# Block products of an FFN on unscaled activations, summed in PSUM, and one more group of them

## The chip, the cores and the metric

The kernel runs on one core of one Trainium2 chip. The metric is device time in microseconds. Three runs of the kernel before gave 1812.3, 1813.72 and 1814.33 us; the median, 1813.72 us, is the time to compare with. The engines are called PE (TensorE: matmuls), DVE (VectorE), ACT (ScalarE), POOL (GpSimd) and SP (SyncE, which here only issues DMAs).

## The reference, cut to what matters

A sequence of 512 rows of 1024 fp32 numbers passes through two layers. Each layer is an FFN, a mixer and a second FFN; the mixers are not touched by the change except in the order of their instructions. An FFN (width 2816) is:

```python
def _rmsnorm(x, gain):
    y = x * lax.rsqrt(jnp.mean(x * x, axis=-1, keepdims=True) + EPS)
    return y * gain
def _swiglu(h, w_gate, w_up, w_down):
    return (jax.nn.silu(h @ w_gate) * (h @ w_up)) @ w_down
# per layer, twice:
h = _rmsnorm(x, ffn_norm[layer])
x = x + 0.5 * _swiglu(h, ffn_w_gate[layer], ffn_w_up[layer], ffn_w_down[layer])
```

The factor rsqrt(...) is one number per row of x. It can be taken out of `h @ w`, and put on the product.

## The kernel before, in words

**Layout and precision.** x lies transposed in SBUF: eight tiles of 128 features x 512 rows. An fp32 product is made of three matmuls: each operand is split into a high part, rounded to the type fp32r by a cast on ACT, and a low part, the difference, by a subtraction on DVE; the products high x high, high x low and low x high are summed in PSUM. A weight tile is loaded (`raw`, 128x1024), split into a tile `whl`, and used from there. The activations of a stage are `hg` tiles, the split of x times gain, without the row factor; the factor, broadcast to 128 partitions, is the tile `rsB`, and is put on a product as it leaves PSUM.

**An FFN.** Its 22 blocks of 128 hidden columns are worked as 11 pairs (called groups here, q = 0 to 10). A plain group is four units (gate and up of two blocks), each of 8 k-tiles x 3 matmuls of 512 columns (`proj_tile`), emptied by a DVE multiplication with `rsB` (`evac`). From q = `CLASSIC` on, a group is worked as two units of block products (`pair`, one for gate and one for up). A unit takes the two 128-column blocks, both halves of the features and both halves of the rows as a 2x2 block product, and makes it from 7 products in the place of 8. For that it needs sums and differences of weight blocks (made by DVE in `feed`, then split: W1, W3, W4 and W2) and of activations (`TA`, `TB`, made in `blocks`). Each of the 7 products is 4 x 3 matmuls of 256 columns. Before the change `blocks` works on normalized activations: it makes them with `rsB`, makes TA and TB from them, and later makes them again, splits them, and overwrites the activation tiles h (called N) with them, so that all 7 products have the row factor inside. The 7 products are added up by DVE from PSUM with the help tiles p1, u2, u3. `CLASSIC = (3, 9)`: the first FFN (f0) uses block products for q = 9 and 10, the three others for q = 3 to 10.

Then silu and product (`gate`), a split, and the down projection in units of 24 matmuls of 512 columns, in batches of three groups (`GROUPS`), which stand between the units of the following groups. `LEAD = (3, 4)` puts three (f0: four) such down units ahead of the first block product. In `ffn_items` this order is written down.

**The order of the work.** All instructions are put in order when the program is built, by a planner (`Clock`, `cost`) that keeps a time for every engine from fixed costs. The main path emits matmuls; after every few of them, `tick` lets other threads put in work: first the feeder (weight loads and splits), then the threads by `PRIO`. A thread that needs an engine asks `on`: for PE it goes on when its inputs have been ready for `SLACK` (1.5 us in f0) by the planner's clock; for DVE when DVE is at most `BACKLOG` ahead. `side` says whether a PSUM bank can be had for such a thread, by the planner's time at which the bank was last read. On the chip each engine runs its instructions strictly in this order and waits on semaphores.

**S5 tables.** During f0 the thread `prep` makes tables for the first mixer (`s5_prepare`): eight steps `gains_of_inputs` and eight `gains_of_outputs`, each with DVE products, four small matmuls or transposes into a side bank (lines 1177 and 1213), an ACT copy and DMAs through SP's queue. The extra SBUF for block products, and the thread `blocks`, start when `prep` has ended (`extra` in `ffn`).

The profile gives line 205 for every operation (a helper issues them all), so groups are told apart by tiles: `ps` PSUM, `whl` and `wh` split weights, `gs` and `us` gate and up results, `p`, `u` the help tiles, `g`, `bt`, `kt` tiles of the tables.

Of the kernel before, what the change touches and what calls it, by code (L numbers as in the profile page):

```python
# [17 lines left out]
P = 128  # L18
S = 512
# [22 lines left out]
CLASSIC = (3, 9)  # L42
LEAD = (3, 4)
HOLD = (1, 0)
# [11 lines left out]
PRIO = {"evac": 0, "gate": 0, "small": 5, "prep": 6, "blocks": 6, "s5_bounce": 1, "s5_quarter": 0, "s5_gate": 0, "s5_eighth": 1,  # L56
# [52 lines left out]
class Clock:  # L109
# [140 lines left out]
class Builder:  # L250
    def __init__(self, ctx, tc, A, out, plan):
# [18 lines left out]
        self.f, self.rsB, self.h, self.ndone, self.reserve, self.then, self.final = None, None, None, 0, 0, None, False  # L270
        self.xhold, self.go = False, False
# [46 lines left out]
    def on(self, eng, *aps, ps=0):  # L318
        c = self.clk
        while True:  # L320
            r = c.ready(*aps)
            if eng == "PE":
                ok = r + SLACK[self.name] <= c.now
            elif eng == "DMA":
                ok = r <= c.now + 0.5
            else:
                ok = r <= c.now + 0.3 and c.t[eng] <= c.now + self.backlog
            if ok and (not ps or self.side(ps) is not None):
                return
            yield  # L330
# [414 lines left out]
    def ffn(self, f, gi, then, prepare=None):  # L745
# [4 lines left out]
        with ExitStack() as st:  # L750
# [7 lines left out]
            def extra():  # L758
# [4 lines left out]
                self.xhold, self.go = prep is None, False  # L763
# [3 lines left out]
            self.N, self.TA, self.TB, self.ndone = h, [], [], 0  # L767
            grown = False
            for key in ffn_items(f):
# [3 lines left out]
                if key[0] == "blocks":  # L773
# [4 lines left out]
                    self.go = True  # L778
# [20 lines left out]
                elif key[0] == "pair":  # L799
                    q, i = key[2:]  # L800
                    self.until(lambda: self.ndone == KD and len(self.TB) == 4)
                    if i == 0:
                        t = {"gs": self.pair(w, "gs")}
                        nc.scalar.activation(out=t["gs"], in_=t["gs"], func=AF.Silu)
                    else:
                        t["us"] = self.pair(w, "us")
                        self.add("gate", self.gate(t, g, q, [1] * 4, 1))
                        if q == NFF // 2 - 1:
                            self.give(*self.N, *self.TA, *self.TB)
                else:  # L810
# [27 lines left out]
    def evac(self, ps, t, tag, m, done):  # L838
        while not self.scaled():
            yield  # L840
        if t[tag] is None:
            yield from self.room(tag, 1)
            if t[tag] is None:
                t[tag] = self.ft.tile([P, 2, S], F32, tag=tag, name=self.n(tag), bufs=1)
            else:
                self.leave(tag)
# [22 lines left out]
    def blocks(self, h, gi, late):  # L869
# [5 lines left out]

        hold = HOLD[late]
        again, kept = range(max(0, 4 - hold)), {}

        def normalized(kk, tag):
            t = yield from self.grab(tag, F32)  # L880
            n = (t[:, 0], t[:, 1]) if tag == "hg" else (t[:, lo], t[:, hi])
            for i in range(2):
                yield from self.normed(n[i], 4 * i + kk, h, gi, late)
            return t, n

        for kk in range(4):
            tn, (n1, n2) = yield from normalized(kk, "raw" if kk in again else "hg")
# [7 lines left out]
            v.tensor_tensor(out=t4, in0=t2, in1=n2[:, a], op=ALU.subtract)  # L895
            if kk in again:
                self.give(tn)
            else:
                kept[kk] = tn, (n1, n2)
# [4 lines left out]
            self.give(rt)  # L904

        for kk in again[:2]:
            kept[kk] = yield from normalized(kk, "raw")
        self.xhold = self.xhold and len(kept) < 4
        for kk in (3, 2, 1, 0):
            while not self.go:  # L910
                yield
            if kk not in kept:
                kept[kk] = yield from normalized(kk, "raw")
                self.xhold = self.xhold and len(kept) < 4
            tn, n = kept[kk]
            for i in range(2):
                yield from self.split_steps(n[i], h[4 * i + kk])
                self.ndone += 1
            self.give(tn)
        self.reserve = 0  # L920

    def block(self, ps, t, at, rhs, c, prev=None):
        nc = self.nc
        for kk in range(4):
            w = slice(at + kk * P, at + kk * P + P)
            r = rhs[kk]
            a = nc.tensor.matmul(out=ps, lhsT=t[:, 0, w], rhs=r[:, 0, c], start=kk == 0, stop=False)
            if kk == 0:
                self.after(a, prev)
            nc.tensor.matmul(out=ps, lhsT=t[:, 0, w], rhs=r[:, 1, c], start=False, stop=False)  # L930
            a = nc.tensor.matmul(out=ps, lhsT=t[:, 1, w], rhs=r[:, 0, c], start=False, stop=kk == 3)
            self.tick()
        return a

    def pair(self, w, tag):
# [4 lines left out]
        add = lambda out, x, y, op=ALU.add: v.tensor_tensor(out=out, in0=x, in1=y, op=op)  # L940
        p1, u2, u3 = (self.ft.tile([P, 256], F32, tag=tag, name=self.n(tag), bufs=1) for tag in ("p1", "u2", "u3"))

        X = self.main_ps()
        a = self.block(X[:, lo], W1, 512, N[4:8], lo)
        self.block(X[:, hi], W1, 0, N[0:4], lo, a)
        self.give(W1)
        self.nc.scalar.copy(out=p1, in_=X[:, hi])
        dst = self.ftile(tag)
        add(dst[:, 0, lo], X[:, lo], p1)
        self.free(X)  # L950
        Y = self.main_ps()
        a = self.block(Y[:, lo], W3, 0, TA, lo)
        self.block(Y[:, hi], W3, 512, TA, hi, a)
        self.give(W3)
        add(u2, Y[:, hi], p1)
        add(dst[:, 0, hi], Y[:, lo], u2)
        Z = self.main_ps()
        a = self.block(Z[:, lo], W4, 512, N[4:8], hi)
        self.block(Z[:, hi], W4, 0, TB, lo, a)
        self.give(W4)  # L960
        add(u3, Z[:, hi], u2)
        add(dst[:, 1, hi], Y[:, lo], u3)
        self.free(Y)
        add(dst[:, 0, hi], Z[:, lo], dst[:, 0, hi])
        self.free(Z)
        V = self.main_ps()
        self.block(V[:, lo], W2, 0, TB, hi)
        self.give(W2)
        add(dst[:, 1, lo], u3, V[:, lo], ALU.subtract)
        self.free(V)  # L970
        return dst
# [73 lines left out]
    def s5_prepare(self, pool):  # L1045
# [115 lines left out]
        def gains_of_outputs(e):  # L1161
# [15 lines left out]
            yield from self.on("PE", g1, bmx, ps=1)  # L1177
# [23 lines left out]
        def gains_of_inputs(e):  # L1201
# [11 lines left out]
            yield from self.on("PE", bt, ps=1)  # L1213
# [877 lines left out]
```

## Time and profile before

| | |
|---|---|
| median of 3 runs | 1813.72 us |
| the profiled execution | 1810.71 us |
| its span, first to last instruction | 1808.7 us |
| busy: PE, DVE, ACT | 99%, 79%, 42% |
| mean granted clock of PE | 0.999 |
| matmuls | 10514 |
| block products: units, matmuls of 256 columns | 52, 4368 |
| HBM read, mean rate | 192.82 MB, 114 GB/s |

The profile is of one execution; its time of 1810.71 us is that of the whole execution, the span is what the profiler saw between the first and the last instruction. A busy PE is not PE at its peak: matmuls overlap, so their durations (392 ns for 512 columns) are longer than the time from one start to the next. A wait is named after the operation that released it.

### The profile page before, as it was taken

The numbers are of one execution on the slowest core, as the hardware profiler recorded it, in microseconds if no ns is written. First come the engines' busy times: TensorE is split into PE (matmuls) and PEld (weight loads), VectorE is DVE, ScalarE is ACT, GpSimd is POOL, SyncE is SP. The second block draws the span as 40 slices with busy tenths as digits, with TensorE's granted clock in tenths as the row PEclk, the third lists the DMA queues.
The fourth block names the chain that finished last, engine by engine and source line by source line (L and its number), as shares of the span: only waits on it lengthen the run. The fifth ranks groups of instructions, "written<-read, shape, count | busy, mean of one in ns | idle before, by whom it ended". The sixth has DMA issues, their size and how long they took to land.

```text
span 1808.7 us, 26795 instructions
## 1 busy us (share of the span) xinstructions
PE 1792.4 (99%) x10514; PEld 1564.3 (86%) x10514; DVE 1428.9 (79%) x2599; ACT 754.7 (42%) x1082; POOL 18.7 (1%) x35
## 2 busy tenths in 40 slices
PE   9999999999999999999999999999999999999999
PEld 7877888978878889999988999998888788999997
DVE  8989877878986878887777988775578678988864
ACT  4323423433574444343343444333466544434331
POOL 0000000000010000000000000000000000000000
PEclk9999999999999999999999999999999999999999
DMA  5247432337773223332422333332434422333331
GB/s 196 92 141 190 144 103 82 117 130 205 201 168 114 88 89 104 118 105 95 138 64 78 106 117 97 103 102 86 144 78 111 129 82 76 100 106 107 111 98 70
DMA packets 80749, 207.16 MB, mean 115 GB/s; under 512 B 18000, under 2 KB 30320, under 8 KB 79472
## 3 DMA queue, kind: packets, MB, share of 16 engines
q1 hardware_dynamic: 78032, 196.52, 34.6%
q0 software_dynamic: 2448, 8.91, 3.1%
q8 instruction: 83, 1.36, 0.3%
q14 instruction: 42, 0.34, 0.1%
q10 hardware_dynamic: 144, 0.02, 0.0%
HBM read 192.82 MB, written 12.60 MB: 114 GB/s over the span
## 4 chain that ended last, share of the span: by engine, by line
PE 88%; DVE 8%; DMA 2%; issue 1%; ACT 1%; SPq 0%; DVEq 0%; ACTq 0%
PE ps L205 88%; DVE whl L205 1%; DVE hg L205 1%; DVE us L205 1%; DVE ex L205 1%; DVE ssb L205 1%; DMA raw<-in_wglu_dram 0%; DMA prm<-prm 0%; DMA s5ys<-ys 0%; ACT whl L205 0%; DVE s5x L205 0%; DMA ssb<-acsd 0%; DVE sc L205 0%; ACT hg L205 0%; DMA raw<-in_wgu_dram 0%
## 5 line engine op out<-in xcount | busy, mean ns | idle before, releaser
L205 PE MATMUL ps<-hg,whl 128*128 128x512 f32 (+1 forms) x8688 | 1609.6, 345 | 5.5 <-DVE hg L205 2.5
L205 PEld LDWEIGHTS ps<-hg,whl 128*128 128x128 f32 x8688 | 1375.5, 190 | 203.8 <-issue 4.6
L205 ACT CAST whl<-raw 128x1024 fp32r<-128x1024 f32 x366 | 383.0, 1051 | 532.3 <-PE ps L205 323.4
L205 DVE TENSOR_TENSOR whl<-raw,whl 128x1024 fp32r<-128x1024 f32 x349 | 424.1, 1222 | 180.8 <-ACT whl L205 180.3
L205 DVE SCALAR_TENSOR_TENSOR x<-ps,x 128x512 f32<-128x512 f32 x128 | 87.1, 688 | 37.0 <-PE ps L205 35.4
L205 DVE TENSOR_TENSOR raw<-raw,raw 128x512 f32<-128x512 f32 (+1 forms) x182 | 111.3, 649 | 2.2
L205 ACT CAST hg<-us 128x512 fp32r<-128x512 f32 x88 | 52.1, 620 | 105.2 <-DVE us L205 104.9
L205 PE MATMUL ps<-hg,wh 128*128 128x256 f32 x624 | 83.4, 283 | 0.0
L205 ACT ACTIVATE gs<-gs 128x1024 f32<-128x1024 f32 x44 | 46.7, 1060 | 85.5 <-DVE gs L205 85.5
L205 PEld LDWEIGHTS ps<-hg,wh 128*128 128x128 f32 x624 | 78.6, 192 | 0.0
L205 DVE TENSOR_TENSOR raw<-raw 128x512 f32<-128x512 f32 (+1 forms) x78 | 46.6, 597 | 16.4 <-DMA raw<-in_wgu_dram 16.4
L205 ACT COPY p<-ps 128x256 f32<-128x256 f32 x52 | 19.3, 372 | 95.5 <-PE ps L205 86.1
L205 DVE TENSOR_TENSOR hg<-us,hg 128x512 fp32r<-128x512 f32 x88 | 57.9, 685 | 0.0
L205 DVE TENSOR_TENSOR us<-gs,us 128x1024 f32<-128x1024 f32 x44 | 53.6, 1219 | 0.4
L205 ACT ACTIVATE hg<-x,gains 128x512 fp32r<-128x512 f32 x48 | 33.6, 722 | 32.4 <-DVE x L205 30.0
L205 ACT CAST hg<-raw 128x512 fp32r<-128x512 f32 x58 | 34.4, 622 | 21.3 <-DVE raw L205 20.6
L205 DVE TENSOR_TENSOR hg<-raw,hg 128x512 fp32r<-128x512 f32 x58 | 38.1, 689 | 0.1
L205 DVE SCALAR_TENSOR_TENSOR hg<-x,gains,hg 128x512 fp32r<-128x512 f32 x48 | 34.9, 746 | 2.5 <-ACT hg L205 2.5
L205 DVE TENSOR_TENSOR wh<-raw,wh 128x512 fp32r<-128x512 f32 x52 | 35.7, 686 | 0.0
L205 DVE TENSOR_TENSOR us<-ps,rsB 128x512 f32<-128x512 f32 x40 | 28.9, 723 | 4.5 <-PE ps L205 4.4
L205 ACT CAST wh<-raw 128x512 fp32r<-128x512 f32 x52 | 32.0, 616 | 0.0
L205 DVE TENSOR_TENSOR acc<-acc,sq 128x512 f32<-128x512 f32 x42 | 29.0, 690 | 0.9
(264 smaller groups left out, 1100.0 us busy)
## 6 DMA issues: line engine op xcount, KB each, us to landing
raw<-in_wgu_dram SPq DMA_DIRECT2D x176, 512.0 KB, 3.6
raw<-in_wdn_dram SPq DMA_DIRECT2D x88, 512.0 KB, 3.6
raw<-in_wev_dram SPq DMA_DIRECT2D x16, 512.0 KB, 3.6
prm<-prm SPq DMA_DIRECT2D x8, 1024.0 KB, 6.9
raw<-in_wod_dram SPq DMA_DIRECT2D x12, 512.0 KB, 3.6
raw<-in_wevo_dram SPq DMA_DIRECT2D x8, 512.0 KB, 6.6
raw<-in_wodo_dram SPq DMA_DIRECT2D x8, 512.0 KB, 6.4
x<-in_xT_dram SPq DMA_DIRECT2D x8, 256.0 KB, 5.6
```

Source lines behind the costliest of these rows:

```text
L205: r = f(*args, **kw)
```

## The change

- `pair` reads the activation tiles as they are (gain, no row factor). The two products of `N` with W1 and the one with W4 are multiplied with `rsB` when DVE reads them from PSUM; TA and TB are still made from normalized activations, so the four other products need no factor. `blocks` no longer makes the normalized activations a second time and no longer writes them back to h.
- Results that are sums of products are accumulated in PSUM: the bank X first holds W1 N[0:4], is read (p1), and then has W1 N[4:8] added; the bank Y is read after each of three products that are added into it in turn. The sign of t4 is turned for this. The last product of a unit is emitted in the next unit, after two blocks of it, or after a down unit (`pending`).
- The first product of a unit no longer waits until all activations are made again; each product waits only until its own TA or TB is there. `blocks` gets priority 0 in the place of 6; a thread `evac` is put behind the others of its priority.
- `CLASSIC = (3, 8)`: f0 uses block products for q = 8 too. `LEAD = (0, 0)`.
- The PE steps of the tables wait for `PREP_SLACK` = 4.0 us in the place of 1.5, for their inputs and for the bank; `side` takes the slack into account for every thread.
- The planner's cost of an fp32r matmul is (n + 32) / 2400 us.
- `WIDE` is False for all FFNs: the wide form in `block` is not used.

```diff
-CLASSIC = (3, 9)
-LEAD = (3, 4)
-HOLD = (1, 0)
+CLASSIC = (3, 8)
+LEAD = (0, 0)
+
+WIDE = (False, False)
...
+PREP_SLACK = 4.0
-PRIO = {... "blocks": 6, ...
+PRIO = {... "blocks": 0, ...
...
             if kw["lhsT"].dtype == F32R:
-                return max(0.11, 0.0025 + n / 2400)
+                return (n + 32) / 2400
...
     def add(self, kind, gen):
-        i = next((i for i, (q, _) in enumerate(self.threads) if q >= p), len(self.threads))
+        i = next((i for i, (q, _) in enumerate(self.threads) if q > p or q == p and kind != "evac"), len(self.threads))
...
-    def on(self, eng, *aps, ps=0):
+    def on(self, eng, *aps, ps=0, slack=None):
+        slack = SLACK[self.name] if slack is None else slack
...
-                ok = r + SLACK[self.name] <= c.now
+                ok = r + slack <= c.now
...
-            if ok and (not ps or self.side(ps) is not None):
+            if ok and (not ps or self.side(ps, slack) is not None):
...
-    def side(self, n=1):
+    def side(self, n=1, slack=0.0):
-            ok = min(most - self.open[w], sum(t <= self.clk.now for t in self.freed[w]))
+            ok = min(most - self.open[w], sum(t + slack <= self.clk.now for t in self.freed[w]))
...
                 elif key[0] == "pair":
                     q, i = key[2:]
-                    self.until(lambda: self.ndone == KD and len(self.TB) == 4)
                     if i == 0:
-                        t = {"gs": self.pair(w, "gs")}
-                        nc.scalar.activation(out=t["gs"], in_=t["gs"], func=AF.Silu)
-                    else:
-                        t["us"] = self.pair(w, "us")
-                        self.add("gate", self.gate(t, g, q, [1] * 4, 1))
+                        t = {}
+                    last = self.pair(w, t, "us" if i else "gs", pending)
+
+                    def pending(last=last, t=t, q=q, i=i):
+                        last()
+                        if i == 0:
+                            nc.scalar.activation(out=t["gs"], in_=t["gs"], func=AF.Silu)
+                        else:
+                            self.add("gate", self.gate(t, g, q, [1] * 4, 1))
...
+                    if pending:
+                        pending()
+                        pending = None
...
     def blocks(self, h, gi, late):
-            tn, (n1, n2) = yield from normalized(kk, "raw" if kk in again else "hg")
+            tn = yield from self.grab("raw")
+            n1, n2 = tn[:, lo], tn[:, hi]
+            for i, n in enumerate((n1, n2)):
+                yield from self.normed(n, 4 * i + kk, h, gi, late)
...
-            v.tensor_tensor(out=t4, in0=t2, in1=n2[:, a], op=ALU.subtract)
+            v.tensor_tensor(out=t4, in0=n2[:, a], in1=t2, op=ALU.subtract)
...
-        for kk in again[:2]:
-            kept[kk] = yield from normalized(kk, "raw")
-        self.xhold = self.xhold and len(kept) < 4
-        for kk in (3, 2, 1, 0):
...
-            for i in range(2):
-                yield from self.split_steps(n[i], h[4 * i + kk])
-                self.ndone += 1
-        self.reserve = 0
+        self.xhold, self.reserve = False, 0

+    def block(self, ps, t, at, rhs, c, more=False, wide=False):
         for kk in range(4):
+            self.until(lambda: len(rhs) > kk)
...
+            first, last = kk == 0 and not more, kk == 3
...
+    def pair(self, w, t, tag, before):
...
         X = self.main_ps()
+        self.block(X, W1, 0, N[0:4], lo)
+        p1 = new("p1", 2)
+        times(p1, X[:, lo], lo)
+        Z = self.main_ps()
+        self.block(Z[:, hi], W4, 512, N[4:8], hi)
+        if before:
+            before()
+        t[tag] = dst = self.ftile(tag)
+        Y = self.main_ps()
+        self.block(Y, W3, 512, TA, hi, wide=wide)
+        plus(dst[:, 0, hi], Y, p1)
+        self.block(X, W1, 512, N[4:8], lo, more=True)
+        times(dst[:, 0, lo], X[:, lo], lo)
+        self.block(Z, W3, 0, TA, lo)
+        add(dst[:, 0, hi], Z[:, lo], dst[:, 0, hi])
+        p5 = new("p5", 1)
+        times(p5, Z[:, hi], hi)
+        add(dst[:, 0, hi], dst[:, 0, hi], p5)
+        self.block(Y, W4, 0, TB, lo, more=True, wide=wide)
+        plus(dst[:, 1, hi], Y, p1)
+        add(dst[:, 1, hi], Z[:, lo], dst[:, 1, hi])
+
+        def last():
+            self.block(Y, W2, 0, TB, hi, more=True, wide=wide)
+            plus(dst[:, 1, lo], Y, p1)
+        return last
...
-            yield from self.on("PE", g1, bmx, ps=1)
+            yield from self.on("PE", g1, bmx, ps=1, slack=PREP_SLACK)
...
-            yield from self.on("PE", bt, ps=1)
+            yield from self.on("PE", bt, ps=1, slack=PREP_SLACK)
```

`times(out, x, c)` multiplies with `rsB[:, c]`, `plus(out, ps, x)` adds `ps[:, 0:256]` and x (not wide), `add` adds; `new` makes a 128x256 help tile.

More of the change, by code (lines that the diff above doesn't have):

```diff
@@ L269, in __init__ @@
         self.raws, self.ahead = [], []
-        self.f, self.rsB, self.h, self.ndone, self.reserve, self.then, self.final = None, None, None, 0, 0, None, False
-        self.xhold, self.go = False, False
+        self.f, self.rsB, self.h, self.reserve, self.then, self.final = None, None, None, 0, None, False
+        self.xhold = False
         self.later = []
@@ L840, in evac @@
             yield
+        while t[tag] is None and self.cnt.get(tag, 0):
+            yield
         if t[tag] is None:
[L842 to L846, printed above, removed]
+            self.cnt[tag] = 1
+            t[tag] = self.ft.tile([P, 2, S], F32, tag=tag, name=self.n(tag), bufs=1)
         yield from self.on("DVE", ps, self.rsB)
@@ L904, in blocks @@
             self.give(rt)
-        for kk in again[:2]:
-            kept[kk] = yield from normalized(kk, "raw")
-        self.xhold = self.xhold and len(kept) < 4
-        for kk in (3, 2, 1, 0):
[L910 to L916, printed above, removed]
-                yield from self.split_steps(n[i], h[4 * i + kk])
-                self.ndone += 1
-            self.give(tn)
-        self.reserve = 0
-    def block(self, ps, t, at, rhs, c, prev=None):
+        self.xhold, self.reserve = False, 0
+    def block(self, ps, t, at, rhs, c, more=False, wide=False):
         nc = self.nc
         for kk in range(4):
+            self.until(lambda: len(rhs) > kk)
             w = slice(at + kk * P, at + kk * P + P)
             r = rhs[kk]
[L927 to L931, printed above, removed]
+            first, last = kk == 0 and not more, kk == 3
+            o = ps[:, 0:256]
+            go = dict(start=first, stop=False, skip_group_check=more)
+            if wide:
+                nc.tensor.matmul(out=ps.rearrange("p (a b) -> p a b", a=2), lhsT=t[:, 0, w], rhs=r[:, :, c], **go)
+            else:
+                nc.tensor.matmul(out=o, lhsT=t[:, 0, w], rhs=r[:, 0, c], **go)
+                go["start"] = False
+                nc.tensor.matmul(out=o, lhsT=t[:, 0, w], rhs=r[:, 1, c], **go)
+            nc.tensor.matmul(out=o, lhsT=t[:, 1, w], rhs=r[:, 0, c], start=False, stop=last, skip_group_check=more)
             self.tick()
-        return a
-    def pair(self, w, tag):
+    def pair(self, w, t, tag, before):
         v = self.nc.vector
@@ L939, in pair @@
         N, TA, TB = self.N, self.TA, self.TB
-        add = lambda out, x, y, op=ALU.add: v.tensor_tensor(out=out, in0=x, in1=y, op=op)
-        p1, u2, u3 = (self.ft.tile([P, 256], F32, tag=tag, name=self.n(tag), bufs=1) for tag in ("p1", "u2", "u3"))
-        X = self.main_ps()
-        a = self.block(X[:, lo], W1, 512, N[4:8], lo)
-        self.block(X[:, hi], W1, 0, N[0:4], lo, a)
+        add = lambda out, x, y: v.tensor_tensor(out=out, in0=x, in1=y, op=ALU.add)
+        times = lambda out, x, c: v.tensor_tensor(out=out, in0=x, in1=self.rsB[:, c], op=ALU.mult)
@@ new lines, in pair, with plus @@
+        new = lambda tag, n: self.ft.tile([P, 256], F32, tag=tag, name=self.n(tag), bufs=n)
+        wide = WIDE[self.f == 0]
+        def plus(out, ps, x):
+            add(out, ps[:, lo], x)
+            if wide:
+                add(out, ps[:, hi], out)
+        X = self.main_ps()
+        self.block(X, W1, 0, N[0:4], lo)
[5 more added lines that the diff above has]
+            before()
```

48 lines of the change are left out of this document (9 added, 39 removed).

## The prediction

> **What bounds the kernel now.** First the page's top.
>
> ```profile
> span 1808.7 us, 26795 instructions
> PE 1792.4 (99%) x10514; PEld 1564.3 (86%) x10514; DVE 1428.9 (79%) x2599; ACT 754.7 (42%) x1082; POOL 18.7 (1%) x35
> ```
>
> PE (TensorE) is busy for 1792.4 of 1808.7 us, so at most 16.3 us can be won without removing matmuls. Busy says nothing of the pace, so the second view is the timeline of PE, in two stretches that hold one shape each.
>
> ```profile
> 214.65 30.54 PE L205 MATMUL ps<-hg,whl 128*128 128x512 f32 x134
> 1029.43 8.80 PE L205 MATMUL ps<-hg,whl 128*128 128x256 f32 x72
> ```
>
> The first column is the start, the second the time from the first start to the last end. A row of n matmuls has n-1 steps and one full duration, which the page gives as 392 and 283 ns. So a 512-column matmul takes (30.54-0.39)/133 = 0.2267 us from start to start, a 256-column one (8.80-0.28)/71 = 0.1200 us. There are no gaps inside either row: here PE runs at its own pace and nothing else sets the time. Where it does not, the list of what PE waited for says it: waited-for, total us, times, longest us.
>
> ```profile
> PE ps L205 <- DVE hg L205: 3.0, 3, 1.5
> PE ps L205 <- DVE us L205: 2.9, 1, 2.9
> PE ps L205 <- DVE ones L205: 1.1, 1, 1.1
> PE ps L205 <- DVE whl L205: 1.1, 2, 0.5
> PE ps L205 <- DMA hg<-s5us: 0.8, 1, 0.8
> PE ps L205 <- DVE pu L205: 0.7, 1, 0.7
> PE ps L205 <- DMA prm<-prm: 0.6, 1, 0.6
> PE ps L205 <- DVE s L205: 0.5, 1, 0.5
> PE ps L205 <- ACT whl L205: 0.5, 1, 0.5
> PE ps L205 <- DVE x L205: 0.2, 1, 0.2
> PE ps L205 <- DVE cr L205: 0.2, 1, 0.2
> ```
>
> All of it is 11.6 us. By the tiles' names: ones and whl (2.7 with ACT's) belong to the start; us (2.9) and x (0.2) to the first FFN; hg, s5us, prm and cr (4.6) to the even mixer; pu and s (1.2) to the odd one. No row names a tile of the block products (p, u, gs, wh), so in the 52 units of these PE never waits. **So three things can move the time: the number and width of matmuls, the 2.9 us wait, and waits that are new.**
>
> **One group more of block products.** A group done plainly is 4 units x 8 k x 3 = 96 matmuls of 512 columns: 96 x 0.2267 = 21.76 us. As block products it is 2 x 7 x 12 = 168 of 256 columns: 168 x 0.1200 = 20.16 us. PE is the bound on both sides, so this is **-1.6 us**. All other FFN matmuls keep number and width: where a block grows in a bank that is already filled, it is still 12 matmuls.
>
> [...]
>
> **The wait of 2.9 us.** The timeline of PE, then that of DVE (VectorE), at this place:
>
> ```profile
> 97.40 0.96 PE L205 MATMUL ps<-hg,whl 128*128 128x512 f32 x3
> 101.22 0.42 PE L205 MATMUL ps<-g,s5bm 128*32 128x128 f32 x8 [2.86 <-DVE us L205]
> ```
>
> ```profile
> 98.62 1.22 DVE L205 TENSOR_TENSOR whl<-raw,whl 128x1024 fp32r<-128x1024 f32 x1
> 99.75 0.69 DVE L205 TENSOR_TENSOR hg<-us,hg 128x512 fp32r<-128x512 f32 x1
> 100.47 0.69 DVE L205 TENSOR_TENSOR us<-ps,rsB 128x512 f32<-128x512 f32 x1
> ```
>
> The matmul of the S5 tables (its wait: line 1177) is not late for its own input: it sits in a PSUM bank that the evacuation us<-ps at 100.47 has still to empty, and every later matmul stands behind it in PE's order. The planner had taken the bank for free. With the change this step, and the transposes behind line 1213, wait until inputs and bank have been free for 4 us in the planner's clock, 2.5 us more than now for the inputs and 4 more for the bank. The actual lateness was 2.9, so 4 covers it: **-2.9 us**. At worst the wait reappears at another step (0).
>
> What that delays: the table work is a chain of 8 + 8 such steps. Its last transposes and its last DMA are these rows of the timelines of PE and of SP's queue.
>
> ```profile
> 183.90 0.60 PE L205 MATMUL ps<-ident,bt 128*128 128x128 f32 x4
> 189.22 0.42 PE L205 MATMUL ps<-g,s5bm 128*32 128x128 f32 x8
> ```
>
> ```profile
> 192.55 3.94 SPq L205 DMA_DIRECT2D prm<-kt  x8
> ```
>
> The chain ends at 196.5. The 8 steps of the input tables run one after the other, so the delay is at most 8 x 2.5 = 20 us (216), at least none; the first step's lateness already paid 2.9 there. I take +8, because several steps wait for more than their slack already (between the last transposes at 183.9 and the last psk at 189.2 lie 5.3 us): end at about 204. The 64 kt DMAs and the loads on SP's queue move with it; the weights ahead are loaded on the same queue, but each of these DMAs holds it only about 0.5 us (3.94 for 8).
>
> **Does the earlier first pair find its operands?** The first copy of a block product starts at 310.5 (row below), after two blocks of 12 x 0.12: the pairs start at 307.4. Ahead of them stood 4 down units of 24 matmuls (21.8 us) and group 8 with its two down units (21.8 + 10.9). So group 8, now the first pair, starts at 307.4 - 54.4 = 253, less the 2.9: 250. Here are the row of that copy, then the stretches before and behind 250 (us; busy time of PE, weight loads, DVE, ACT, POOL; clock; DMA), then DVE's groups between 196 and 310.
>
> ```profile
> L205 ACT COPY p<-ps x52: 352/373/378, 310.5 to 1769.9; 128x256 f32<-128x256 f32 x52
> ```
>
> ```profile
> 200.00:250.00 50.00, 50.00 (x222) 41.40 (x221) 48.12 (x74) 18.39 (x23) 0.00 (x0) 1.00 0.35 117
> 250.00:282.00 32.00, 32.00 (x143) 26.49 (x142) 11.59 (x13) 8.33 (x9) 0.00 (x0) 1.00 0.34 99
> ```
>
> ```profile
> L205 DVE TENSOR_TENSOR whl<-raw,whl 128x1024 fp32r<-128x1024 f32 x22 | 26.9, 1222 | 23.9 <-ACT whl L205 23.9
> L205 DVE TENSOR_TENSOR raw<-raw,rsB 128x512 f32<-128x512 f32 x16 | 11.1, 692 | 0.6
> L205 DVE TENSOR_TENSOR raw<-hg 128x512 f32<-128x512 f32 x16 | 11.0, 686 | 0.1
> L205 DVE TENSOR_TENSOR hg<-raw,hg 128x512 fp32r<-128x512 f32 x16 | 10.5, 687 | 0.0
> L205 DVE TENSOR_TENSOR raw<-raw,raw 128x256 f32<-128x256 f32 x8 | 3.4, 423 | 0.1
> L205 DVE TENSOR_TENSOR raw<-raw 128x256 f32<-128x256 f32 x8 | 3.3, 418 | 0.0
> ```
>
> Half of each 512-wide row is the pass that makes TA and TB, half the renormalizing and re-splitting that the change drops; the 256-wide rows stay. So the pass is 11.1/2 + 11.0/2 + 10.5/2 + 6.7 = 23 us of DVE, and 16.3 us of DVE (and 8 casts of ACT) are gone. Today the pass runs from 200.9 to 240.9 at the lowest priority, on a DVE that is 96% busy (48.12 of 50). In the new order it starts near 204 with first rank, and needs about the same: 244. The four weights of the first pair now fall into the same 50 us: 4 sums of 0.69, three splits of 1.22 and one of 0.69, 7.1 us, in the place of the two renormalizations that ran by 250 (8 of those ops, 5.5 us). DVE is then full to 250, and has 20 us to spare in the stretch behind it. PE asks for TA only 2 x 1.44 us after the pair starts, for TB after 5 x 1.44. I take **0**, with 9 us as the other end (first rival). In the other three FFNs nothing delays the pass, its cover is the whole of groups 0 to 2 (65 us of PE), and dropping the 3 down units ahead costs nothing there: **0**.
>
> **The products themselves.** A unit's 7 DVE adds and one ACT copy become 9 DVE operations, all 128x256. Two of today's groups (of the second FFN's pairs) and two stretches there:
>
> ```profile
> L205 DVE TENSOR_TENSOR u<-ps,p 128x256 f32<-128x256 f32 x16 | 6.7, 422 | 1.7 <-PE ps L205 1.7
> L205 DVE TENSOR_TENSOR us<-u,ps 128x256 f32<-128x256 f32 x8 | 3.3, 415 | 0.4 <-PE ps L205 0.4
> ```
>
> ```profile
> 660.00:707.00 47.00, 47.00 (x368) 45.89 (x367) 43.38 (x68) 19.17 (x25) 0.00 (x0) 1.00 0.31 97
> 707.00:832.00 125.00, 125.00 (x872) 117.34 (x871) 102.16 (x154) 50.20 (x63) 0.00 (x0) 1.00 0.35 108
> ```
>
> Two more of 0.42 us in each unit of 10.1 us (with its down unit 15.5 us) take DVE from 102.16/125 = 82% to 87% in a steady stretch. Today's first four units come without down units between them (660 to 707: DVE 92%, and no wait of PE); without the lead each unit is followed by a down unit, so that crowding goes. What is new is that a bank is read in the middle of its growth: the second block into X waits for p1, the second into Y for the first sum out of it, the third for the next. Between the read and the next write stand two blocks, 2.88 us; for the third a whole down unit. Ahead of a read DVE can hold one split (1.22) and two sums (0.69 each) at a backlog, 2.6 us, and the read itself is 0.42: 3.0 against 2.88, so the cover is just enough, and gone when ACT's cast is late too. Bounds: 0, and 2 x 0.15 us in each of the 54 units, 16 us. As the groups show DVE idling for PE before such sums (1.7 us before u<-ps,p), rather than the other way round, I take near the lower end: **+0.6 us**.
>
> **The planner's clock** now charges a matmul (n+32)/2400, which is what the rows above measure (0.2267, 0.1200); it charged 0.2158 and 0.1100. Everything placed "so many us later" falls 5 to 9% fewer matmuls later, in the mixers too. Bounds: their 5.8 us of waits gone, or as much again. No row prefers either sign: **0**.
>
> **Sum.** -1.6 - 2.9 + 0.6 = -3.9 us. The profiled execution took 1810.71 us (span 1808.7 and 2.0 around it) and would take 1806.8; it lies 3.0 below the median of the runs, 1813.72, so the forecast is **1809.8 us**.
>
> **The rivals.**
>
> *The tables come too late in the first FFN (slower).* Place: the first pair of f0. If the chain pays its full 2.5 us eight times, it ends at 216; the pass at today's pace of 40 us ends at 256, and with the pair's 7.1 us ahead of it on a full DVE at 263. PE then stands from 254 (two blocks and three quarters of the third behind 250): 9 us. -3.9 + 9 = +5.1, **1818.8**. It decides from a pass that ends at 258 (no gain left); past 262 the time is worse by over 0.2%. For it: DVE at 96%. Against: the 20 us of room at 250, first rank for the pass, and chain steps that already wait longer than their slack.
>
> *The growing banks make PE wait.* The wait that goes is replaced by many small ones: 0.15 us in half of 54 units' two places gives 4 us, and the gain is eaten: **1813.5**. For it: the cover of 2.88 against 3.0. Against: no wait of the kind in 52 units today.
>
> *The wait moves.* The bank of the tables' step stays guarded by a clock that errs elsewhere, and only the group remains: -1.6 + 0.6, **1812.7**.
>
> *The better clock helps the mixers* by half of their 5.8 us: **1806.9**.
>
> **How the numbers follow.** A measurement of this kernel tells a difference of about 0.2% (3.6 us, 1810.1) from none. Chances: forecast 0.42 (own range 1808 to 1811.5, two thirds of it beyond 0.2%), late tables 0.15, growing banks 0.17, moved wait 0.12, mixers helped 0.14. Faster: 0.28 + 0.14 + 0.03 of the others = 0.45; slower: 0.15 + 0.02 of the growing banks, whose upper bound is far = 0.17; within: 0.38. The range 1805 to 1817.5 leaves out the worse half of the late tables and the far ends.
>
> **What would show it.** PE's waits: the row with us (2.9) gone, none naming p, u, gs or X's banks; 10,586 matmuls instead of 10,514 (+168 - 96). The row p<-ps leaves ACT, the re-splits hg<-raw,hg fall from 58 to 32. The first 256-column matmul near 250 instead of 307, with no idle in it. Wrong would be: idle time of PE at 250 to 265 waiting for DVE hg or whl; PE waits by DVE p, gs or us spread over the pairs; or mixer stretches that differ by more than 2 us.

## The result, and the profile after

The change makes the kernel slower. Four runs took 1886.96 to 1891.81 us, median 1890.51, against 1813.01 for the kernel before on the same chip: **+77.5 us, a ratio of 1.0417 (95% interval 1.0400 to 1.0434)**. The forecast was 1809.8, with 1817.5 as the upper end of its range. The profiled execution took 1890.09 us.

The top of its page, with the rows of PE's busy tenths and of PE's granted clock over 40 slices of 47 us:

```profile
span 1888.4 us, 26804 instructions
...
PE 1820.2 (96%) x10586; PEld 1581.2 (84%) x10586; DVE 1431.4 (76%) x2662; ACT 722.2 (38%) x1002; POOL 18.6 (1%) x35
...
PE   9999999999999799999987999999999978999999
...
PEclk9999999999999899999998999999999989999999
```

PE has the 72 matmuls more that were forecast. The span grew by 79.7 us: idle time of PE went from 16.3 to 68.2 us, and its busy time by 27.8 although the added group should have saved 1.6. The holes stand in three places, and the clock dips in the same ones. What PE waited for (waited-for, total us, times, longest us):

```profile
PE ps L207 <- DVE gs L207: 30.8, 11, 4.3
PE ps L207 <- DVE us L207: 21.4, 3, 7.1
PE ps L207 <- DVE p L207: 2.7, 2, 1.3
```

The first two rows are the loss, and they name tiles of the *plain* groups: gs and us are written by `evac`, which empties the bank of a plain unit. The growing banks of the pairs (p) cost 2.7 us in the whole kernel. Three stretches hold the loss, the plain groups at the start of the second, third and fourth FFN. Columns: stretch; its us; busy us (and instructions) of PE, weight loads, DVE, ACT, POOL; granted clock; DMA share; GB/s. First the kernel after, then the same first stretch before:

```profile
600.00:660.00 60.00, 43.38 (x163) 34.21 (x162) 36.71 (x59) 17.39 (x22) 0.00 (x0) 0.86 0.19 61
960.00:1030.00 70.00, 53.38 (x217) 42.68 (x216) 42.42 (x73) 18.13 (x24) 0.00 (x0) 0.88 0.19 60
1520.00:1585.00 65.00, 48.38 (x184) 38.34 (x183) 37.33 (x66) 17.77 (x22) 0.00 (x0) 0.84 0.19 57
```

```profile
600.00:660.00 60.00, 60.00 (x267) 49.67 (x265) 51.53 (x77) 28.18 (x38) 0.00 (x0) 1.00 0.25 86
```

In each of the three PE idles 16.6 us, together 49.9. It waits for DVE, yet DVE is *less* busy than before (36.7 against 51.5 us) and idles 23 us itself. No engine is full; they wait for each other in a ring. The timelines show one turn of it (start, us, engine, operation, count, idle before and its releaser). PE of the kernel after:

```profile
610.04 7.30 PE L207 MATMUL ps<-hg,whl 128*128 128x512 f32 x24 [3.66 <-DVE gs L207]
624.46 7.34 PE L207 MATMUL ps<-hg,whl 128*128 128x512 f32 x24 [7.12 <-DVE us L207]
636.14 13.70 PE L207 MATMUL ps<-hg,whl 128*128 128x512 f32 x48 [4.33 <-DVE gs L207]
```

PE does one unit of 24 matmuls, ends at 617.3, and stands for 7.12 us until a bank is empty. ACT in that time:

```profile
617.42 1.04 ACT L207 CAST whl<-raw 128x1024 fp32r<-128x1024 f32 x1 [8.61 <-PE ps L207]
```

And DVE:

```profile
613.47 0.42 DVE L207 TENSOR_TENSOR raw<-raw,raw 128x256 f32<-128x256 f32 x1
618.50 1.23 DVE L207 TENSOR_TENSOR whl<-raw,whl 128x1024 fp32r<-128x1024 f32 x1 [4.61 <-ACT whl L207]
619.64 1.29 DVE L207 TENSOR_TENSOR hg<-raw,hg 128x512 fp32r<-128x512 f32 x2
620.84 1.41 DVE L207 SCALAR_TENSOR_TENSOR raw<-x,gains,rsB 128x512 f32<-128x512 f32 x2
...
623.63 0.68 DVE L207 TENSOR_TENSOR us<-ps,rsB 128x512 f32<-128x512 f32 x1
```

Read it in this order. The end of PE's unit at 617.3 gives back a weight buffer; only then can ACT cast the next weight into it (617.42, after 8.61 us of nothing to do). DVE has stood before the split of that weight for 4.61 us. Behind the split, in DVE's order, come splits of TA and TB (619.64) and operations of the pass of `blocks` (620.84 and four more), and behind those the evacuation us<-ps (623.63), whose inputs had been ready since 617.3 at the latest. With it PE's next bank comes free, at 624.3, and PE starts at 624.46. So one evacuation of 0.68 us stands behind a weight that waits for PE, and PE stands behind the evacuation.

The two edits responsible for this order are in the text of the change: `blocks` has priority 0 like `evac`, and a new `evac` is put *behind* the threads of its priority. The pass is asked first, and when it has put DVE more than 1.5 us ahead in the planner's clock (`BACKLOG` of these FFNs), `evac` isn't let on at all.

The rest of the loss goes with the clock: granted were 0.77, 0.77 and 0.80 over the three rows of PE above. The 24 matmuls from 624.46 took 7.34 us; at the pace of before they take 23 x 0.2267 + 0.39 = 5.60, so 1.7 are lost. The row above it loses 1.7 too, the one below 13.70 - 11.05 = 2.7: some 6.1 us in the second FFN. The same three rows take 7.30, 7.04 and 13.59 us in the third and lose 5.7, and 8.24, 7.44 and 13.76 us in the fourth and lose 7.2. With the 49.9 us of idle time that is 69 us.

### The profile page after: what moved, and what is told of

Its sections match the earlier page's. It is cut to its first block, busy times and chain, and to the rows that moved or that the text cites. A ratio compares the mean times of both kernels' runs of the same rounds, so it can differ in the third digit from the quotient of the medians.

```text
span 1888.4 us, 26804 instructions
## 1 busy us (share of the span) xinstructions
PE 1820.2 (96%) x10586; PEld 1581.2 (84%) x10586; DVE 1431.4 (76%) x2662; ACT 722.2 (38%) x1002; POOL 18.6 (1%) x35
## 4 chain that ended last, share of the span: by engine, by line
PE 80%; DVE 12%; issue 4%; ACT 2%; DMA 1%; SPq 0%; ACTq 0%; DVEq 0%
PE ps L207 80%; DVE whl L207 3%; DVE raw L207 2%; DVE hg L207 1%; ACT whl L207 1%; DVE us L207 1%; DMA raw<-in_wgu_dram 1%; DVE s_t L207 1%; DVE gs L207 1%; DVE ex L207 0%; ACT hg L207 0%; DVE s5x L207 0%; DVE ssb L207 0%; DVE sc L207 0%; DMA x<-in_xT_dram 0%
## 5 line engine op out<-in xcount | busy, mean ns | idle before, releaser
L207 PE MATMUL ps<-hg,whl 128*128 128x512 f32 (+1 forms) x8736 | 1632.2, 347 | 58.6 <-DVE gs L207 30.8
L207 DVE TENSOR_TENSOR raw<-raw,raw 128x512 f32<-128x512 f32 (+1 forms) x194 | 117.1, 643 | 2.4
L207 PEld LDWEIGHTS ps<-hg,wh 128*128 128x128 f32 x648 | 84.9, 191 | 4.2
L207 DVE TENSOR_TENSOR raw<-raw 128x512 f32<-128x512 f32 (+1 forms) x86 | 50.5, 587 | 40.1 <-DMA raw<-in_wgu_dram 40.0
L207 DVE TENSOR_TENSOR us<-ps,rsB 128x512 f32<-128x512 f32 (+1 forms) x65 | 39.0, 600 | 17.8 <-PE ps L207 17.6
L207 DVE TENSOR_TENSOR gs<-ps,p 128x256 f32<-128x256 f32 x81 | 34.0, 420 | 20.5 <-PE ps L207 18.7
L207 DVE TENSOR_TENSOR p<-ps,rsB 128x256 f32<-128x256 f32 x108 | 45.0, 417 | 5.5 <-PE ps L207 5.5
L207 DVE TENSOR_TENSOR us<-ps,p 128x256 f32<-128x256 f32 x81 | 34.0, 419 | 17.5 <-PE ps L207 17.5
L207 ACT ACTIVATE hg<-x,gains 128x512 fp32r<-128x512 f32 x48 | 33.7, 720 | 32.1 <-DVE x L207 29.6
L207 DVE TENSOR_TENSOR gs<-ps,rsB 128x512 f32<-128x512 f32 (+1 forms) x61 | 34.5, 566 | 1.6 <-PE ps L207 1.0
```

The source lines that it names most:

```text
L207: r = f(*args, **kw)
```

## The experiments

Differences are taken to the median of the kernel before, run beside each experiment on the same chip (1811.8 to 1813.1 us). "The order" below stands for the theory just told.

### The order of pass and evacuation

**e1_rank6** puts the pass back to its old priority, behind the evacuations.

```diff
-PRIO = {... "blocks": 0, ...
+PRIO = {... "blocks": 6, ...
```

> The changed kernel with one number put back: the thread blocks has priority 6 again, behind evac. Theory A (the pass that makes TA and TB stands ahead of evac in the order of the threads, takes DVE each time its backlog falls under 1.5 us, and so the evacuations of the plain units come too late and PE waits for a bank): PE's waits for gs and us in the plain groups of the last three FFNs (16.6 us each) go, and the half clock behind them; time 1890 - 72 = 1815 to 1822 us. Theory B (the first pairs, now without the lead of down units, come before their weights and tables; the rank has nothing to do with it): the waits stay or grow, 1885 us or more. Theory C (a rank of 6 makes the tables late for the first pair, the price of the dropped lead): the waits move from the plain groups to the first pair of each FFN, 1825 to 1860 us.

**e2_evac_first** leaves it at 0 and puts new threads ahead of equals again, as before.

```diff
-        i = next((... if q > p or q == p and kind != "evac"), ...
+        i = next((... if q >= p), ...
```

> The changed kernel with one condition put back: a new thread, evac too, stands ahead of the others of its priority; blocks keeps priority 0. Theory A in its narrow form (only the order of evac and blocks decides, not the early start of the pass): the waits for gs and us in the plain groups go and the time is 1810 to 1820 us, the same as with blocks at priority 6 within 4 us. If it is the load that the early pass puts on DVE, not the order, the waits stay above 10 us in each FFN and the time above 1850 us.

**e3_before_rank0** makes the two edits alone, on the kernel before.

```diff
-PRIO = {... "blocks": 6, ...
+PRIO = {... "blocks": 0, ...
-        i = next((... if q >= p), ...
+        i = next((... if q > p or q == p and kind != "evac"), ...
```

> The kernel before with only these two edits of the change: blocks at priority 0 and evac behind the others of its priority. Theory A: the same starving of the evacuations appears without any of the new products, 1865 to 1890 us, with waits of PE for gs and us in the plain groups of the last three FFNs. Theory B (it takes the new products or the dropped lead): 1810 to 1818 us.

**e4_backlog** keeps the order and lets DVE threads on until DVE is 2.5 us ahead.

```diff
-BACKLOG = {... "f1": 1.5, "f2": 1.5, ... "f3": 1.5}
+BACKLOG = {... "f1": 2.5, "f2": 2.5, ... "f3": 2.5}
```

> The changed kernel with the allowed backlog of DVE at 2.5 us in all four FFNs (1.5 in the last three as changed, 2.5 in the first, where no such wait is seen). If the backlog is what lets the evacuations of the first FFN through in spite of the same rank, the waits for gs and us fall under 6 us in each FFN and the time to 1815 to 1840 us. If the first FFN is spared for another reason (its pass begins when the plain groups have run for long, and not at the start of an FFN with nothing evacuated yet), the waits stay: 1875 to 1900 us.

Measured: e1 1821.44 us (ratio 1.0055, 1.0038 to 1.0072), e2 1821.79 (1.0052, 1.0037 to 1.0067), e3 1846.79 (1.0188, 1.0163 to 1.0213), e4 1829.81 (a single run). As differences: +8.4, +8.7, +33.7 and +16.7. So either edit undone takes back some 69 us of the 77.5, and the two alone cost the kernel before 33.7 us. In e2 the stretch is closed at full clock:

```profile
600.00:660.00 60.00, 60.00 (x295) 50.90 (x294) 51.27 (x78) 26.03 (x32) 0.00 (x0) 1.00 0.29 88
```

In e3 PE has the same waits as in the kernel after, fewer of them, in the second and the fourth FFN and not in the third. The time stays below the 1865 us that were expected, so on the kernel before the two edits alone do not cost what they cost in the changed one; the next section has a reason.

```profile
PE ps L205 <- DVE gs L205: 12.8, 4, 3.3
PE ps L205 <- DVE us L205: 11.6, 3, 4.4
```

e4 shows that it is the limit that shuts `evac` out: with 1 us more of it, and the pass still first, all three stretches close. The first of them, and what PE waited for instead:

```profile
600.00:660.00 60.00, 60.00 (x298) 51.07 (x297) 51.22 (x78) 24.95 (x32) 0.00 (x0) 1.00 0.33 97
```

```profile
PE ps L207 <- DVE p L207: 12.4, 8, 2.1
```

A deeper backlog on DVE lets the growing banks wait: 12.4 us for p, against 3.6 in e2. That is the forecast's rival of the growing banks, and it is 12 us only at this backlog. That undoing the order takes back 68.8 us (77.5 - 8.7) is shown, by e2 and by e1. Left are 8.7 us (e2), and the planner's cost of a matmul was the next suspect.

### The planner's cost

**e5_old_cost** is e2 with the old cost.

```diff
-                return (n + 32) / 2400
+                return max(0.11, 0.0025 + n / 2400)
```

> The changed kernel with evac ahead of blocks (as in e2_evac_first) and the planner's old cost of an fp32r matmul, max(0.11, 0.0025 + n/2400). Theory D (the cost that agrees with the measured pace takes away a hidden margin of 5 to 9%: steps of the mixers are placed after fewer matmuls, and PE meets them too early): PE's waits between 378 and 560 us fall from 7.4 to about 4.6 us, the half clock at 546 goes, and the time falls from 1821.8 to about 1816 us. Rival (the mixer's waits come from the new order at the end of the first FFN, not from the cost): 1820 to 1823 us.

**e6_before_new_cost** is the kernel before with the new cost, **e9_after_old_cost** the kernel after with the old one, and **e10_rank6_old_cost** is e5 with `blocks` at 6.

```diff
# e6, on the kernel before
-                return max(0.11, 0.0025 + n / 2400)
+                return (n + 32) / 2400
# e9, on the kernel after
-                return (n + 32) / 2400
+                return max(0.11, 0.0025 + n / 2400)
# e10, on e5
-PRIO = {... "blocks": 0, ...
+PRIO = {... "blocks": 6, ...
```

> The kernel before with the planner's new cost of a matmul alone. Theory D: waits in the even mixer grow as they did in the change, 1816 to 1820 us. The prediction's own value for this edit was 0: 1812 to 1814 us.

> The changed kernel with the planner's old cost of a matmul alone; evac stays behind blocks. If the two causes add up, the order of the threads costs what it cost with the new cost, 69 us, and the time is 1814 + 69 = 1883 us. If the new cost makes the starving worse (with the old one the planner's PE runs ahead of the real one, DVE's backlog falls under the limit sooner, and evac gets more turns), it is nearer to the 34 us that the same two edits cost the kernel before: about 1848 us.

> Evac ahead of blocks, the old cost, and blocks at priority 6. PE waited 3.7 us for p in the first pair of the first FFN with blocks at priority 0, because the pass stood ahead of the weights' sums and of p on DVE. If the rank of the pass makes that wait, it falls under 1 us and the time to 1811 us; if DVE is simply full there, the pass only ends later, the wait becomes one for hg of the tables, and the time stays at 1814 us or grows to 1820 us.

Measured: e5 1814.44 (1.0009, 0.9999 to 1.0019), e6 1824.04 (1.0060, 1.0040 to 1.0080), e9 1852.0 (a single run), e10 1812.59 (1.0004, 0.9995 to 1.0013). As differences to before:

| | evacuation first | pass first |
|---|---|---|
| new cost | e2: +8.7 | after: +77.5 |
| old cost | e5: +2.3 | e9: +39.6 |

The new cost adds 6.4 us in the left column, 37.9 in the right, and 11.9 on the kernel before (e6), though it is the cost that the timelines confirm (0.2267 and 0.1200 us). The two causes overlap: of the 77.5 us the order alone undone takes back 68.8, the cost alone 37.9 (by one run), both together 75.2. In e5 the waits of the even mixer fall as theory D expected, further even: from 7.4 us in e2 to 2.7 (hg 1.8, s5us 0.7, cr 0.2, between 378 and 565 us). The waits of e6 that were not there before, or smaller:

```profile
PE ps L205 <- DVE bt L205: 4.5, 2, 3.0
PE ps L205 <- DMA prm<-prm: 2.4, 1, 2.4
PE ps L205 <- DMA hg<-s5us: 2.2, 1, 2.2
PE ps L205 <- DVE x L205: 2.2, 4, 1.0
```

bt and x belong to the first FFN, prm and s5us to the even mixer: steps that are put in "so many us later". With a dearer matmul, the planner puts fewer matmuls between a step and its inputs. The first transposes of the tables show it, in the kernel before and in e6:

```profile
96.52 0.60 PE L205 MATMUL ps<-ident,bt 128*128 128x128 f32 x4
```

```profile
90.08 0.66 PE L205 MATMUL ps<-ident,bt 128*128 128x128 f32 x4 [2.96 <-DVE bt L205]
```

In e6 PE comes to them at 87.1 and waits for bt; in the kernel before it comes at 96.5 and does not wait. The old cost was too low by 5 to 9%, and for these steps that was a margin. That the same holds for the steps of the mixer, where e6 also has another order of instructions than the kernel before, is a reading and not shown. That the new cost also makes the starving twice as dear is measured (in the old row by one run, e9); how (a planner that thinks PE slower falls under the DVE limit less often) is only argued.

**The rank with the old cost.** e10 stands at +0.2 and e5 at +2.3, and PE's wait in the first pair is shorter in e10, but not under 1 us:

```profile
257.03 11.38 PE L207 MATMUL ps<-hg,whl 128*128 128x256 f32 x60 [2.31 <-DVE p L207]
```

In e5 this wait is 3.66 us (below). So the rank of the pass makes a part of it, some 1.3 us, and 2.3 us stay without it. Neither of the two expectations is met in full.

### The group, the slack and the backlog of the first FFN

**e7_before_classic8** is the kernel before with one group more; **e8_f0_backlog** is e2 with the shorter backlog in the first FFN; **e11_classic9** is e5 without the added group; **e12_slack8** is e5 with the table steps waiting twice as long; **e13** has both, and **e14** one group fewer than before as well.

```diff
# e7, on the kernel before
-CLASSIC = (3, 9)
+CLASSIC = (3, 8)
# e8, on e2
-BACKLOG = {"f0": 2.5, ...
+BACKLOG = {"f0": 1.5, ...
# e11, on e5
-CLASSIC = (3, 8)
+CLASSIC = (3, 9)
# e12, on e5; e13, on e11
-PREP_SLACK = 4.0
+PREP_SLACK = 8.0
# e14, on e13
-CLASSIC = (3, 9)
+CLASSIC = (3, 10)
```

> The kernel before with one group more of block products in the first FFN, in the old form, and nothing else (the lead of four down units is cut to the two that are there). The prediction's term: 72 matmuls more, PE's pure time 1.6 us less, 1811.5 us, if the pass that makes the tables ends in time. If the first pair comes before its operands (the prediction's first rival), PE waits for hg or whl near 275 us and the time is 1815 us or more.

> The changed kernel with evac ahead of blocks, and the allowed backlog of DVE in the first FFN at 1.5 us in the place of 2.5. Theory E (a bank that grows is read in time only if little stands ahead of the read on DVE: at 2.5 us PE waited 3.1 us for p in the two pairs at 290 and 328 us of the first FFN, and 12.4 us in all with 2.5 us in every FFN): the waits for p in the first FFN fall under 1 us, time 1818 to 1820 us. If the waits come from the order in which gate and weight sums are put in, not from the backlog, they stay at about 3 us: 1821 to 1823 us.

> Evac ahead of blocks, the old cost, and the first FFN with two groups of block products as before the change. The new form of the products alone then stands against the old. If the first pair's wait of 3.7 us belongs to the earlier group, it goes here, the group's own 1.6 us are lost, and the time is 1812 us; the group itself was then worth -1.6 + 3.7 = +2.1 us. If the wait belongs to the new form (a bank that is read while it grows), it stays: 1816 us.

> Evac ahead of blocks, the old cost, and the table steps 8 us behind their inputs and banks in the place of 4. With 4 us the wait of 2.9 us did not go, it moved by some matmuls to the next plain unit, which waits 2.4 us for us<-ps, the same evacuation. If the bank is short because the table step takes it while evacuations are 4 us behind the planner's clock, 8 us let the evacuation through first: the wait falls under 0.5 us and with it the half clock behind it, 1811 us. If the tables' work on DVE itself holds the evacuations back, the wait stays at 2 to 3 us: 1814 us.

> Evac ahead of blocks, the old cost, block products of the first FFN from group 9 as before the change, and the table steps 8 us behind their inputs and banks. With 8 us the wait of 2.4 us near 99 us went, but the tables ended later and the first pair, which then came at 252 us, waited 9.2 us for them. If both halves hold (the wait is gone, and a pair that comes 30 us later finds its operands), this is e11_classic9 less 2.4 us and the half clock behind it: 1808 to 1809.5 us, faster than the kernel before by 0.2%. If something else waits in the place of it, 1811 us or more.

> The same with one group of block products in the first FFN in the place of two. With nothing late, one group more or less is worth its matmuls alone: 96 x 0.2267 - 168 x 0.1200 = 1.6 us by the pace of the kernel before, so 1.6 us slower than e13_classic9_slack8. If the 256-column matmuls bring DVE work that makes PE wait, the difference is nearer to 0 or turns.

| | median, us | ratio (95%) | to before |
|---|---|---|---|
| e7 | 1820.92 | 1.0041 (1.0029 to 1.0054) | +8.8 |
| e8 | 1821.43 | 1.0044 (1.0030 to 1.0058) | +9.3 |
| e11 | 1811.07 | 0.9996 (0.9986 to 1.0005) | -1.3 |
| e12 | 1819.05 | 1.0036 (1.0023 to 1.0049) | +6.7 |
| e13 | 1818.70 | 1.0039 (1.0026 to 1.0053) | +6.9 |
| e14 | 1807.00 | 0.9970 (0.9959 to 0.9982) | -4.8 |

**The group.** With it e5 stands at +2.3, without it e11 at -1.3: it costs some 3.6 us in the place of saving 1.6 (each of the two intervals is nearly 2 us wide to either side). What PE waited for in e5:

```profile
PE ps L207 <- DVE p L207: 4.8, 3, 3.7
PE ps L207 <- DVE us L207: 2.4, 1, 2.4
```

The 3.7 is one place, the first pair; e11 has the same 2.4 us for us and none for p. DVE's timeline there:

```profile
254.54 1.28 DVE L207 TENSOR_TENSOR hg<-raw,hg 128x512 fp32r<-128x512 f32 x2
...
256.46 1.90 DVE L207 TENSOR_TENSOR raw<-raw,raw 128x512 f32<-128x512 f32 x3
258.28 1.22 DVE L207 TENSOR_TENSOR whl<-raw,whl 128x1024 fp32r<-128x1024 f32 x1
259.41 0.41 DVE L207 TENSOR_TENSOR p<-ps,rsB 128x256 f32<-128x256 f32 x1
```

The read of the growing bank, 0.41 us, stands behind splits and sums of later weights. In the kernel before the group is dearer still (e7): there the pair needs all activations made again, and PE stands at its start for 7.6 and then 2.6 us, the longest waits of these rows:

```profile
PE ps L205 <- ACT hg L205: 7.6, 1, 7.6
PE ps L205 <- DVE hg L205: 4.4, 3, 2.6
```

So the new form does make an early pair cheaper (3.6 against 8.8), but with the old cost DVE, which the pass and the weights share, does not read the bank in time at 250 us.

**The slack.** With 8 us of it (e12) the 2.4 us wait for us is gone, but the tables end at 213 us instead of 206, and the first pair stands twice:

```profile
255.95 0.80 PE L207 MATMUL ps<-hg,whl 128*128 128x256 f32 x2 [4.08 <-DVE hg L207]
261.85 13.30 PE L207 MATMUL ps<-hg,whl 128*128 128x256 f32 x63 [5.11 <-ACT hg L207]
```

That is 9.2 us, the first rival of the forecast at its place and its price (9 us), released by another 4 us of slack. The time of e12, 1819.05, lies above both of its expectations, which had not asked what the later end does to the first pair.

**The backlog.** With 1.5 us in the first FFN (e8) no read of a growing bank waits there any more, but the table steps do (rows of the stretch from 60 to 380 us), and the time is that of e2 within its interval:

```profile
PE ps L207 <- DVE bt L207: 2.8, 1, 2.8
PE ps L207 <- DVE us L207: 1.7, 1, 1.7
```

**e13 and e14.** With the first pair some 30 us later (280.8 instead of 251.8 in e5), tables that end later should cost nothing there, and PE waits only 0.7 us in the first FFN behind 60 us. The two kernels differ by one group of the first FFN. These are the first matmuls of the even mixer, behind the same work, in e13 and then in e14:

```profile
376.92 5.01 PE L207 MATMUL ps<-hg,wdt 128*8 128x512 f32 x21
```

```profile
377.73 5.24 PE L207 MATMUL ps<-hg,wdt 128*8 128x512 f32 x22
```

In the first FFN behind 60 us e14 has no wait of PE, e13 that one of 0.7 us, for p. So the group brings e13 to the mixer 0.8 us earlier, 1.5 without that wait: a group whose operands are in time is worth what the pace says, -1.6. Yet e13 stands 8.2 us above e11, and 11.7 above e14. Its new waits are in the even mixer:

```profile
PE ps L207 <- DMA whl<-in_wev_dram: 3.2, 1, 3.2
PE ps L207 <- DVE ysq L207: 2.4, 1, 2.4
PE ps L207 <- DVE hg L207: 2.0, 1, 2.0
```

The stretch of the even mixer in e13, and then in e14:

```profile
370.00:565.00 195.00, 184.28 (x1068) 148.98 (x1067) 152.85 (x378) 96.65 (x159) 7.79 (x9) 0.96 0.60 173
```

```profile
370.00:565.00 195.00, 191.37 (x1120) 154.44 (x1119) 160.47 (x387) 98.41 (x163) 7.79 (x9) 1.00 0.65 184
```

e13 has 7.1 us more of idle time here and a clock of 0.96 against 1.00 (over the 184 us of busy time that loses up to 7 us, an estimate from this row). From the first matmul of the mixer to the first pair of the second FFN e13 takes 274.9 us and e14 263.0: 11.9, the whole difference between the kernels. Both have 1426 matmuls in between; by tiles and shapes e14 and e11 have them in the same order, e13 in another after the first 21. So the loss of e13 is the order of its mixer, which the planner makes anew when an edit ahead of it shifts the time. Why this one order is bad stays open. e14, with the evacuations first, the old cost, a slack of 8 us and one group *fewer* than before, is faster than both kernels: 1807.0 us, though its expectation was 1.6 us slower than e13. By the two rows above, leaving out the group is not what makes it faster; its trace has no wait of PE in the first FFN behind 60 us and a mean granted clock of 1.0. Which of its edits is worth how much of the 4.8 us was not tried.

## Why the prediction was wrong, step by step

**The step that failed** is "In the other three FFNs nothing delays the pass, its cover is the whole of groups 0 to 2 ... and dropping the 3 down units ahead costs nothing there: 0". It asks what delays the pass, and not whom the pass delays. Its DVE work is covered in sum (DVE idles 23 of 60 us in the starved stretch), but with first rank it stands ahead of the evacuations that PE needs. The term should have been +68.8 with the new cost (what e2 takes back), +37.3 with the old one (e9 less e5, where e9 is one run). It could have been read from the change: both edits are listed there, and `evac` is the thread that empties PE's banks. None of the four rivals held it; the late tables and the growing banks looked for DVE's load, not its order.

**The planner's clock**, taken as 0 because "No row prefers either sign", measured +6.4 with the evacuations first and +11.9 alone on the kernel before. Its bounds were "their 5.8 us of waits gone, or as much again"; the loss was beyond them on the kernel before. That waiting fewer matmuls takes margin away was an argument for that sign, and was left out. The cost also moves the tables, which the forecast had not joined: they end at 186.9 us in e2 and at 206.0 in e5, which differ by the cost alone.

**The wait of 2.9 us** moved, the third rival: with 4 us of slack the table's step is in time, and PE stands at the next plain unit, 2.4 us in e5 and 2.1 in the kernel after. Only the 8 us of e12 to e14 remove it.

**One group more**: the count was right (10,586 matmuls), and in the kernel after itself the first pair starts at 254 us and PE does not wait in it, as forecast. But that is luck: the tables ended at 187.8 us there, not at the forecast 204, because of the new cost. With the old cost they end at 206.0 (e5), and then the step "DVE is then full to 250, and has 20 us to spare in the stretch behind it" fails: +3.6 in the place of -1.6, and in e12 the 9 us of the other end. The -1.6 itself is right by e13 and e14.

**The growing banks** (+0.6) were sized too small, and of the right kind: 2.7 us for p in the kernel after, in two places of the first FFN, where DVE may be 2.5 us ahead; none in the three FFNs where it may be 1.5 ahead, and 12.4 in e4. The rival's price has a slip of its own: 0.15 us in half of the 54 units' two places is 8.1 us, not 4.

**Right**, by these rows: the copies of ACT are gone and DVE does them, from 257 instead of 310; the re-splits fell to 32. The rows of the kernel after:

```profile
L207 DVE TENSOR_TENSOR p<-ps,rsB x108: 411/416/426, 257.2 to 1854.9; 128x256 f32<-128x256 f32 x108
```

```profile
L207 DVE TENSOR_TENSOR hg<-raw,hg 128x512 fp32r<-128x512 f32 x32 | 20.7, 684 | 0.0
```

The forecast without the group and the clock is -2.9 + 0.6 = -2.3, and e11, which leaves out both, measured -1.3; its interval (-2.5 to +0.9) holds both -2.3 and no change. Even an agreement would be luck: the wait that the -2.9 stands for is still there in e11, with 2.4 us. `LEAD` was not tried alone.

## What to carry to other kernels

When work gets a new rank on an engine that runs in order, ask of every operation now behind it who waits for its end; above all an evacuation of PSUM, short itself (0.68 us here), has PE behind it (for 7.12 us), and an average of free time on that engine (23 of 60 us) says little. A cost in a planner that is wrong can be a margin: correct it together with the slack that it carried. And when an edit ahead of a long stage that a planner puts in order moves the time by some us, look first whether that stage itself came out in another order.

## What the hardware did that was not expected

A short wait can cost more than its length: behind some waits of this case the granted clock of PE was lower, down to 0.50. In the kernel before already, behind the 2.86 us wait of the first FFN; the row of these matmuls, and the stretch with its granted clock (0.50, behind the counts):

```profile
101.58 3.35 PE L205 MATMUL ps<-hg,whl 128*128 128x512 f32 x7
```

```profile
101.60:105.00 3.40, 3.40 (x12) 2.72 (x9) 3.16 (x21) 2.08 (x5) 0.00 (x0) 0.50 0.66 230
```

Seven matmuls take (3.35 - 0.39)/6 = 0.49 us each on average instead of 0.2267. With a granted clock of 0.50 for 3.4 us the loss behind this wait is some 1.7 us, so the 2.9 us wait of the forecast had cost some 4.6 us. In the kernel after, the 24 matmuls behind 3.66 and behind 7.12 us lose 1.7 each (granted clock 0.77), and the 48 behind 4.33 us lose 2.7 (0.80). With waits of 2.1 us and of 1.5 us there, the shorter loses nothing:

```profile
98.08 6.21 PE L207 MATMUL ps<-hg,whl 128*128 128x512 f32 x19 [2.12 <-DVE gs L207]
...
651.33 3.88 PE L207 MATMUL ps<-hg,whl 128*128 128x512 f32 x16 [1.50 <-DVE gs L207]
```

6.21 - (18 x 0.2267 + 0.39) = 1.7 at a granted clock of 0.73, and 3.88 - (15 x 0.2267 + 0.39) = 0.1 at 1.00. But the length alone does not decide. In e11 a longer wait at nearly the same place costs nothing more than itself:

```profile
101.31 5.04 PE L207 MATMUL ps<-hg,whl 128*128 128x512 f32 x21 [2.38 <-DVE us L207]
```

5.04 - (20 x 0.2267 + 0.39) = 0.1, so the half clock that the expectation of e13 counts behind this wait does not show in e11. What else decides was not tested, so 1.7 us is a risk behind such a wait and no fixed price.
